# A tenth ring slot for the weights of experts, in space from a smaller DMA scratch and from the tile of router weights; weights in whole tiles

## The chip, the core and the metric

The kernel runs on one core of a Trainium2 chip. The metric is the device time of one execution in microseconds (us). Before the change three runs took 2025.5, 2029.56 and 2029.66 us, median 2029.56. Times inside an execution come from a profiled execution that took 2025.04 us.

## The reference

Two blocks on 512 tokens of width 1024, all in float32. The first mixes a chunked state-space layer and windowed attention, then adds a mixture of 64 experts; the second mixes neighbourhood attention and gated linear attention, then adds a squared-ReLU layer. The part that matters is the experts:

```python
group_logits = t @ w_router_group            # 8 groups
exp_logits = t @ w_router_expert             # 8 experts in each
g_sel = argmax(group_logits)
top_logit, top_local = top_k(exp_logits[g_sel], 2)
gate = softmax(top_logit) * softmax(group_logits)[g_sel]
def expert_block(xb, e):
    hid = silu(xb @ w_gate[e]) * (xb @ w_up[e])     # 1024 -> 512
    return hid @ w_down[e]                          # 512 -> 1024
y = sum over the two chosen experts of gate * expert_block(t, e)
```

Each token goes to two experts of one group. The weights of all 64 experts, 3 matrices of 2 MiB each, are read once: 403 MB of the 494 MB that the execution moves.

## The kernel before

Work in the first block ends with the product with `w_out` (`wout_tail`, L379), tile of 128 tokens by tile; behind each tile comes its share of the routing (`route_tile`, L786, with the router's weights `wr`, and `choose`, L854). Then `experts` (L963) goes over 32 pairs of experts. For a pair, with up to 64 tokens for each expert, PE multiplies with the two gate matrices (L986, two halves of PE's columns side by side), with the two up matrices, turns the result, and multiplies with the two down matrices; between up and down it adds earlier results back to their tokens (`combine`, L1181). The rows of tokens are fetched by GpSimd with an indirect transfer (`fetch`, L841) one or two pairs ahead.

Weights come through a ring. `ring` (L113) takes the next slot and issues loads on SP's queue (`load`, L140: `parts` pieces of equal size, all 128 partitions each; L149). A slot holds one matrix, 16 KiB in each partition. There are nine slots during the experts: three of `ringp` (numbers 0, 1, 6), two of `ring2` (2, 3), two in `A1` and `A2`, which held the first block's normed input (4, 5, named `w16x`), and two of `ring3` (7, 8). Tile k goes to slot k mod 9. `ring3` is opened in `moe` (L729) on the space of the closed pools of the first block (`small1`, `wsp1`, `mix1`), so its first loads wait for the last readers and writers there. Six tiles serve a pair, in the order gate, gate, up, up, down, down; tile numbers in this text count them from 0 to 191. SP's instructions run in order, so a load that waits holds all later ones back. The number of pieces `n` is 4 for experts 0 to 11 (tiles 0 to 35) and 2 after (tiles 36 to 183); expert 2's and 3's gate tiles (6 and 7) take 8; the last four gate and up tiles and the last two down tiles (184 to 187, 190, 191) go through `pair` (L131), which mixes the pieces of two tiles.

A tile program orders the instructions of each engine from their dependencies; a load into a slot waits for the readers of the slot's last content, and for an earlier transfer whose completion semaphore it takes over. Eight such semaphores, DMAHW0 to DMAHW7, serve the transfers of SP and ScalarE in turn.

At the end `Begin` (L1756) starts the second block inside the last pair: it loads `wv` into slot 6 (L1793), and `wsplit` (L152) casts it on ScalarE.

Of the kernel before, what the change touches and what calls it, by code (L numbers as in the profile page):

```python
# [6 lines left out]
FT = mybir.dt.float32  # L7
# [21 lines left out]
class Net:  # L29
# [6 lines left out]
    def setup(self, ctx):  # L36
        tc, nc = self.tc, self.nc
        self.per = ctx.enter_context(tc.tile_pool(name="per", bufs=1))
        self.ringp = ctx.enter_context(tc.tile_pool(name="ring", bufs=3))
        self.dram = ctx.enter_context(tc.tile_pool(name="dram", bufs=1, space=bass.MemoryType.DRAM))  # L40
        self.ps = ctx.enter_context(tc.tile_pool(name="ps", bufs=1, space=PSUM))
        self.rings = [self.ringp]

        per = self.per
        self.H = per.tile([P, NT, D], FT, name="H")
        ones = self.ones = per.tile([P, P], FT, name="ones")
        nc.gpsimd.memset(ones, 1.0)
        self.warm(AF.Sqrt)

        def tri(name, pattern, cmp, base=0, cm=0, fill=0.0, src=None, n=P):  # L50
            t = per.tile([P, n], FT, name=name)
            nc.gpsimd.affine_select(t, ones[:, :n] if src is None else src, pattern=pattern, compare_op=cmp,
                                    fill=fill, base=base, channel_multiplier=cm)
            return t
        self.ident = tri("ident", [[1, P]], OP.is_equal, 0, -1)
        self.upto = tri("upto", [[1, P]], OP.is_ge, 0, -1)
        self.after = tri("after", [[-1, P]], OP.is_gt, 0, 1)
        self.before = tri("before", [[1, P]], OP.is_gt, 0, -1)


        i = self.ins
        self.col = {}

        def columns(name, queue, names):
            rows = per.tile([P, P], FT, name="rows")
            nc.gpsimd.memset(rows, 0.0)
            r = 0
            for n, k in names:
                queue.dma_start(rows[r:r + k, :], dap(i[n], 0, [[P, k], [1, P]]))
                r += k  # L70
            p = self.psum()
            self.pin(nc.tensor.transpose(p[:, :P], rows, self.ident))
            cols = per.tile([P, r], FT, name="c" + name)
            nc.vector.tensor_copy(cols, p[:, :r])
            r = 0
            for n, k in names:
                self.col[n] = cols[:, r:r + k]
                r += k
        self.columns = columns
        columns("a", nc.scalar, (("norm_mix", 8),))  # L80
# [32 lines left out]
    def ring(self, shape, dma, parts=1):  # L113

        self.nring = getattr(self, "nring", -1) + 1
        n = [p.bufs for p in self.rings]
        m = self.nslots = sum(n) + (0 if self.held is None else 2)
        k = self.nring % m
        t = (self.held or {}).get(k)
        if t is None:  # L120

            p = self.rings[0 if self.held is None else (0, 0, 1, 1, 0, 0, 0, 2, 2)[k]]
            if self.held is not None and k in (4, 5):
                t = self.per.tile([P, 4096], FT, name="w16x", tag=("A1", "A2")[k - 4])
            else:
                t = p.tile([P, 4096], FT, name="w16", tag="w16")
            if self.held is not None:
                self.held[k] = t
        return self.load(t, shape, dma, parts)
# [300 lines left out]
    def attention1(self, small, pool, kp, wp, w_in, A, mixes, rsa, kv):  # L430
# [22 lines left out]
        for j in range(8):  # L453
# [31 lines left out]
            if j == 0:  # L485
                p = self.proj(kv[1], A)
                vT = kp.tile([P, T], FT, name="vT", tag="dT", bufs=1)
                self.copy(vT, p)
                p = self.psum()
                for c in range(NT):  # L490
                    nc.tensor.transpose(p[:, c * P:(c + 1) * P], vT[:, c * P:(c + 1) * P], self.ident)
                v = pool.tile([P, NT, P], FT, name="v", bufs=1)
                self.copy(v.rearrange("p c d -> p (c d)"), p)
                self.setup_rest()
                self.router_weights()
            nm = small.tile([P, 2, NT], FT, name="nm", bufs=2)
            nc.vector.tensor_scalar(nm, mx, -1.0, None, op0=OP.mult)
            for hh in range(2):
# [230 lines left out]
    def moe(self, keep, then=None):  # L729

        tc = self.tc
        with ExitStack() as ctx:

            self.nring, self.held = -1, {}
            self.rings = [self.ringp, self.ring2, ctx.enter_context(tc.tile_pool(name="ring3", bufs=2, reuse_waits="tile"))]
            with tc.tile_pool(name="experts", bufs=2, reuse_waits="tile") as pool:
                with ExitStack() as inner:
                    front = inner.enter_context(tc.tile_pool(name="front", bufs=2, reuse_waits="tile"))
                    self.experts(keep, pool, front, inner, then and (lambda: then(inner)))
            self.rings, self.held = [self.ringp], None  # L740
        self.show("h1m", self.H)

    def router_weights(self):
        nc, i, per = self.nc, self.ins, self.per
        g8 = self.g8 = per.tile([P, KT], FT, name="g8")
        nc.gpsimd.dma_start(g8, i["norm_ffn"][0].rearrange("(p j) -> p j", j=KT))
        wr = self.wr = per.tile([P, KT, 72], FT, name="wr")
        nc.gpsimd.dma_start(wr[:, :, :8], i["w_router_group"][0].rearrange("(j p) n -> p j n", p=P))
        nc.gpsimd.dma_start(wr[:, :, 8:], i["w_router_expert"][0].rearrange("(j p) n -> p j n", p=P))
        nc.gpsimd.tensor_tensor(wr, wr, self.col["norm_ffn"].unsqueeze(2).to_broadcast([P, KT, 72]), OP.mult)  # L750

    def route_start(self, keep, pool):
# [13 lines left out]
        self.ones16 = pool.tile([P, P], BF, name="ones16", bufs=1)  # L766
        nc.gpsimd.tensor_copy(self.ones16, self.ones)
        self.before16 = pool.tile([P, P], BF, name="before16", bufs=1)
        nc.gpsimd.tensor_copy(self.before16, self.before)
        self.lg = pool.tile([P, NT, 72], FT, name="lg", bufs=1)  # L770
        self.M = None
        self.ex = keep.tile([P, NT, 8], FT, name="ex")
# [190 lines left out]
    def experts(self, keep, pool, front, inner, then):  # L963
# [5 lines left out]
        wd = i["w_down"][0].rearrange("e (p j) n -> e p j n", j=4)  # L969

        def weights(e0):
            n = 4 if e0 < 12 else 2
            one = lambda shape, w, e: [self.ring(shape, w[e + s], 8 if e == 2 and w is wg else n) for s in range(2)]
            up, dn = [P, KT, 512], [P, 4, D]
            if e0 == 60:

                late.extend((lambda: one(dn, wd, 60), lambda: self.pair(dn, (wd[62], wd[63]))))
                return [(one(up, wg, 60), one(up, wu, 60), None),
                        (self.pair(up, (wg[62], wg[63])), self.pair(up, (wu[62], wu[63])), None)]
            return [(one(up, wg, e0), one(up, wu, e0), one(dn, wd, e0))]  # L980
# [7 lines left out]
        def chosen(q):  # L988

            us = slice(256 * (q % 2), 256 * (q % 2) + 256)  # L990
            km = front.tile([P, 2, NT], FT, name="km", bufs=1)
            V.tensor_scalar(km, self.keys, -4096.0 * (q // 2), None, op0=OP.add)
            for c in range(NT):
                eq = front.tile([P, 256], FT, name="eq", bufs=1)
                V.tensor_scalar(eq, it[:, us], km[:, 0, c:c + 1], None, op0=OP.is_equal)
                V.scalar_tensor_tensor(self.S0[:, c, :], it[:, us], km[:, 1, c:c + 1], eq, op0=OP.is_equal, op1=OP.add)

        def values(q):

# [519 lines left out]
    def gla_gates(self, pool, zT):  # L1519
# [8 lines left out]
        def block(name, src, scale):  # L1528
# [2 lines left out]
            nc.gpsimd.memset(t[0:64, 64:], 0.0)  # L1531
            nc.gpsimd.memset(t[64:, 0:64], 0.0)
            return t
        frm = tmp("frm")[:, :P]
        nc.gpsimd.affine_select(frm, self.ones, pattern=[[-1, P]], compare_op=OP.is_ge, fill=0.0, base=0, channel_multiplier=1)
        s = 1.0 / 16
        cum = (block("upto2", self.upto, s), block("from2", frm, s))
        rest = (block("after2", self.after, s), block("before2", self.before, s))
        mask = (block("mf", self.upto, 1.0), block("mb", self.after, 1.0))

        la = [one(f"la{d}", [P, NT, 256]) for d in range(2)]
# [214 lines left out]
class Begin:  # L1756
# [27 lines left out]
    def norms(self):  # L1784
# [11 lines left out]
        for c in range(NT):  # L1796
            for n in range(2):
                if n:
                    (nc.gpsimd if c == 1 else V).tensor_tensor(h[:, c, :], h[:, c, :], self.gf, OP.mult)
                x = self.pool.tile([P, D], BF, name="x2")  # L1800
                if n and c == 3:
                    V.tensor_tensor_reduce(x, h[:, c, :], h[:, c, :], 1.0, 0.0, OP.mult, OP.add, s[:, 1, c:c + 1])
                else:
                    net.behind.append(nc.scalar.activation(x, h[:, c, :], AF.Square, accum_out=s[:, n, c:c + 1]))

        V.tensor_scalar(s, s, 1.0 / D, None, op0=OP.mult)
# [6 lines left out]
def body(tc, ins, out, dbg=None, stage="all"):  # L1813
    with ExitStack() as ctx:
# [10 lines left out]
        if stage == "moe":  # L1825
            with ExitStack() as ctx2:
                keep = net.moe_pools(ctx2)
                with tc.tile_pool(name="route", bufs=2, side="right", reuse_waits="tile") as pool:
                    net.router_weights()
                    net.route_start(keep, pool)  # L1830
                    net.route(keep, lambda each: [each(c) for c in range(NT)])
                net.moe(keep)
# [35 lines left out]
```

## Time and profile before

| | |
|---|---|
| profiled execution | 2025.04 us |
| its span, first to last instruction | 2023.3 us |
| PE busy | 1928.0 us (95%) |
| VectorE (DVE) busy | 946.3 us (47%) |
| ScalarE (ACT) busy | 534.7 us (26%) |
| GpSimd (POOL) busy | 191.2 us (9%) |
| DMA moved | 494.24 MB, 244 GB/s over the span |
| SP's queue (q1) | 483.63 MB, 60.0% of 16 engines' span |
| GpSimd's transfers (q0) | 6.96 MB, 1.5% |
| mean granted PE clock | 0.989 |

A row of the timeline gives start, duration, engine (SPq is SP's DMA queue), the kernel's line, the operation, what it writes `<-` reads, the number of merged instructions, and in brackets how long the engine had been idle and what ended that. A row of waits gives total us, number of times, longest. A row of a DMA queue gives packets, MB and the share of the 16 DMA engines' time in the stretch. A row of a line gives the number of instructions, shortest/median/longest duration in ns, and the first and last start. Matmul ends are modelled, so a busy PE is not a PE at its peak.

### The profile page before, as it was taken

The numbers are of one execution on the slowest core, as the hardware profiler recorded it, in microseconds if no ns is written. First come the engines' busy times: TensorE is split into PE (matmuls) and PEld (weight loads), VectorE is DVE, ScalarE is ACT, GpSimd is POOL, SyncE is SP. The second block draws the span as 40 slices with busy tenths as digits, with TensorE's granted clock in tenths as the row PEclk, the third lists the DMA queues.
The fourth block names the chain that finished last, engine by engine and source line by source line (L and its number), as shares of the span: only waits on it lengthen the run. The fifth ranks groups of instructions, "written<-read, shape, count | busy, mean of one in ns | idle before, by whom it ended". The sixth has DMA issues, their size and how long they took to land. (4 is left out here: it accounts for less than half of the span.)

```text
span 2023.3 us, 24002 instructions
## 1 busy us (share of the span) xinstructions
PE 1928.0 (95%) x9535; PEld 1209.0 (60%) x9535; DVE 946.3 (47%) x1891; ACT 534.7 (26%) x900; POOL 191.2 (9%) x245
## 2 busy tenths in 40 slices
PE   7999999999999999999999899999999999999998
PEld 5788777734444344343343344348767788888886
DVE  6764667733543243253243243235656654444355
ACT  5773445311010000000000000024443343223232
POOL 5211333110000000000000000002201010000000
PEclk9999999999999999999999999999999999999999
DMA  7312022799999999999999999984212112313211
GB/s 204 115 43 83 32 81 97 268 343 415 415 425 425 424 424 424 424 424 425 424 423 423 421 424 422 422 335 87 92 42 84 43 52 84 125 48 119 103 64 42
DMA packets 114777, 494.24 MB, mean 244 GB/s; under 512 B 16492, under 2 KB 23091, under 8 KB 74984
## 3 DMA queue, kind: packets, MB, share of 16 engines
q1 hardware_dynamic: 107720, 483.63, 60.0%
q0 software_dynamic: 6352, 6.96, 1.5%
q10 hardware_dynamic: 592, 2.10, 0.3%
q8 instruction: 76, 1.25, 0.3%
q14 instruction: 37, 0.30, 0.0%
HBM read 500.68 MB, written 6.15 MB: 250 GB/s over the span
## 5 line engine op out<-in xcount | busy, mean ns | idle before, releaser
L986 PE MATMUL pj<-w,xg 128*64 128x512 f32 x1696 | 467.8, 603 | 47.1 <-DMA w<-in_w_up 45.8
L986 PEld LDWEIGHTS pj<-w,xg 128*64 128x64 f32 x1696 | 152.5, 139 | 334.0 <-issue 257.5
L159 DVE TENSOR_TENSOR wL<-w,wH 128x1024 fp32r<-128x1024 f32 x135 | 167.4, 1241 | 201.1 <-ACT wH L158 198.4
L158 ACT CAST wH<-w 128x1024 fp32r<-128x1024 f32 x136 | 142.3, 1048 | 336.3 <-PE pj L179 163.9
L1091 DVE SCALAR_TENSOR_TENSOR hid<-pj,slots,hid 128x512 f32<-128x512 f32 x30 | 22.5, 751 | 426.8 <-PE pj L986 412.4
L1190 DVE TENSOR_TENSOR H<-sc,H 128x512 f32<-128x512 f32 x248 | 156.5, 683 | 6.2 <-PE sc L1187 3.5
L986 PE MATMUL pj<-w16x,xg 128*64 128x512 f32 x352 | 153.7, 619 | 0.9 <-DMA w16x<-in_w_gate 0.9
L1187 PE MATMUL sc<-yH,ST 128*128 128x512 f32 x256 | 112.7, 440 | 0.6 <-DVE H L1190 0.6
L843 POOL DMA_INDIRECT rows<-hd,tok x31 | 31.7, 1022 | 817.1 <-DVE gates L837 574.3
L1100 ACT COPY hT<-tp 128x512 f32<-128x512 f32 x32 | 18.8, 587 | 339.9 <-PE tp L1098 339.9
L180 PE MATMUL pj<-n3H,wL 128*128 128x512 f32 (+1 forms) x272 | 103.6, 381 | 0.8 <-DVE wL L159 0.8
L178 PE MATMUL pj<-n3H,wH 128*128 128x512 f32 (+1 forms) x272 | 103.6, 381 | 0.0
L179 PE MATMUL pj<-n3L,wH 128*128 128x512 f32 (+1 forms) x272 | 103.5, 380 | 0.0
L178 PE MATMUL pj<-A,wH 128*128 128x512 f32 x240 | 97.3, 405 | 4.0 <-ACT wH L158 2.8
L1187 PE MATMUL sc<-yL,ST 128*128 128x512 f32 x252 | 99.9, 396 | 0.0
L178 PE MATMUL sc<-wH,mixH 128*128 128x512 f32 x252 | 98.5, 391 | 0.4 <-ACT wH L158 0.4
L179 PE MATMUL sc<-wL,mixH 128*128 128x512 f32 x252 | 98.4, 390 | 0.1
L180 PE MATMUL sc<-wH,mixL 128*128 128x512 f32 x252 | 98.2, 390 | 0.0
L179 PE MATMUL pj<-A,wH 128*128 128x512 f32 x240 | 96.8, 403 | 0.0
L180 PE MATMUL pj<-A,wL 128*128 128x512 f32 x240 | 96.2, 401 | 0.5 <-DVE wL L159 0.5
L986 PE MATMUL y<-w,hT 128*64 128x512 f32 x336 | 78.0, 599 | 0.7 <-DMA w<-in_w_down 0.7
L986 PE MATMUL tp<-w,hT 128*64 128x512 f32 x336 | 76.5, 592 | 0.0
(586 smaller groups left out, 3279.6 us busy)
## 6 DMA issues: line engine op xcount, KB each, us to landing
w<-in_w_up SPq DMA_DIRECT2D x88, 1024.0 KB, 20.8
w<-in_w_gate SPq DMA_DIRECT2D x84, 1024.0 KB, 19.6
w<-in_w_down SPq DMA_DIRECT2D x70, 1024.0 KB, 19.6
w16x<-in_w_down SPq DMA_DIRECT2D x32, 1024.0 KB, 20.2
w<-in_w_ff SPq DMA_DIRECT2D x16, 2048.0 KB, 7.8
w<-in_w_in SPq DMA_DIRECT2D x12, 2048.0 KB, 10.4
w<-in_w_up SPq DMA_DIRECT2D x40, 512.0 KB, 9.9
w16x<-in_w_gate SPq DMA_DIRECT2D x20, 1024.0 KB, 19.8
```

What stands on the lines that cost most here:

```text
L158: a = nc.scalar.copy(H, src)
L159: b = (engine or nc.vector).tensor_tensor(L, src, H.bitcast(FT), OP.subtract)
L178: m = mm(out, lH, rH, start=first, stop=False)
L179: mm(out, lH, rL, start=False, stop=False)
L180: mm(out, lL, rH, start=False, stop=last)
L843: self.nc.gpsimd.indirect_dma_start(out=rows, out_offset=None, in_=self.hd[:, :], in_offset=bass.IndirectOffsetOnAxis(ap=tok, axis=0), bou ...
L986: return self.pin(nc.tensor.matmul(*a, **k))
L1091: V.scalar_tensor_tensor(hid, pu, r, hid, op0=OP.mult, op1=OP.mult)
L1100: nc.scalar.copy(hT.rearrange("p j s -> p (j s)"), p)
L1187: m = nc.tensor.matmul(p, ST[:n, t * P:(t + 1) * P], y[:n], start=k == 0, stop=k == len(mms) - 1)
L1190: nc.vector.tensor_tensor(h[:, t, hs], p, h[:, t, hs], OP.add)
```

## The change

The ring gets a tenth slot: a third buffer of `ring3` (slot 9), so tile k goes to slot k mod 10. Its 16 KiB per partition come from a smaller scratch for GpSimd's transfers (4096 bytes of each partition; the default is 16384), from `wr`, which moves from the lasting pool into `small1`, and from smaller tiles: the triangle `before` is made where it is used, `eq` in `chosen` is written into `S0` itself, and the scratch output `x2` of the second block's norms has one buffer, not two (its last use writes `gf`). Loads come in 2 pieces for experts 0 to 7 (tiles 0 to 23) and in one piece for the others; `pair` and the 8 pieces of tiles 6 and 7 stay.

```diff
-            p = self.rings[0 if self.held is None else (0, 0, 1, 1, 0, 0, 0, 2, 2)[k]]
+            p = self.rings[0 if self.held is None else (0, 0, 1, 1, 0, 0, 0, 2, 2, 2)[k]]
...
-            self.rings = [self.ringp, self.ring2, ctx.enter_context(tc.tile_pool(name="ring3", bufs=2, reuse_waits="tile"))]
+            self.rings = [self.ringp, self.ring2, ctx.enter_context(tc.tile_pool(name="ring3", bufs=3, reuse_waits="tile"))]
...
-        wr = self.wr = per.tile([P, KT, 72], FT, name="wr")
+        wr = self.wr = pool.tile([P, KT, 72], FT, name="wr", bufs=1)
...
-        nc.gpsimd.tensor_copy(self.before16, self.before)
+        before = pool.tile([P, P], FT, name="before", bufs=1)
+        nc.gpsimd.affine_select(before, self.ones, pattern=[[1, P]], compare_op=OP.is_gt, fill=0.0, base=0, channel_multiplier=-1)
+        nc.gpsimd.tensor_copy(self.before16, before)
...
-            n = 4 if e0 < 12 else 2
+            n = 2 if e0 < 8 else 1
...
-                eq = front.tile([P, 256], FT, name="eq", bufs=1)
-                V.tensor_scalar(eq, it[:, us], km[:, 0, c:c + 1], None, op0=OP.is_equal)
-                V.scalar_tensor_tensor(self.S0[:, c, :], it[:, us], km[:, 1, c:c + 1], eq, op0=OP.is_equal, op1=OP.add)
+                S = self.S0[:, c, :]
+                V.tensor_scalar(S, it[:, us], km[:, 0, c:c + 1], None, op0=OP.is_equal)
+                V.scalar_tensor_tensor(S, it[:, us], km[:, 1, c:c + 1], S.bitcast(FT), op0=OP.is_equal, op1=OP.add)
...
-                x = self.pool.tile([P, D], BF, name="x2")
                 if n and c == 3:
-                    V.tensor_tensor_reduce(x, h[:, c, :], h[:, c, :], 1.0, 0.0, OP.mult, OP.add, s[:, 1, c:c + 1])
+                    V.tensor_tensor_reduce(self.gf, h[:, c, :], h[:, c, :], 1.0, 0.0, OP.mult, OP.add, s[:, 1, c:c + 1])
                 else:
+                    x = self.pool.tile([P, D], BF, name="x2", bufs=1)
...
-    nc = bacc.Bacc("TRN2", target_bir_lowering=False, num_devices=1)
+    nc = bacc.Bacc("TRN2", target_bir_lowering=False, num_devices=1, dynamic_dma_scratch_size=4096)
```

In `gla_gates` of the second block the triangle is made on GpSimd in the same way, one more select there and one fewer in the setup.

SP's queue where the ring is full for the first time. Before (`w_3921` is slot 7, `w_3930` slot 8, `w_3736` and `w_3741` slots 0 and 1; rows of 512 elements are 2 KiB in each partition, of 1024 4 KiB, and so on; in brackets what the load waits for):

```order
L149 DMA w_3921<-in_w_gate 128x512 [waits DMASW1_49,DMASW5_49,DMASW0_49,DMAHW4_49,DVE_49,Activation_49]
...
L149 DMA w_3930<-in_w_up 128x1024 [waits DMAHW5_49]
L149 DMA w_3930<-in_w_up 128x1024 [waits DMAHW6_49]
L149 DMA w_3930<-in_w_up 128x1024 [waits DMAHW7_49]
L149 DMA w_3930<-in_w_up 128x1024 [waits DMAHW0_49]
L149 DMA w_3736<-in_w_up 128x1024 [waits DMAHW1_49,PE_49]
L149 DMA w_3741<-in_w_down 128x1024 [waits DMAHW2_49,PE_49]
```

Now (`w_3905` is slot 7, `w_3914` slot 8, `w_3917` the new slot 9, `w_3736` slot 0):

```order
L148 DMA w_3905<-in_w_gate 128x512 [waits DMASW3_49,DMASW1_49,DMASW4_49,DMASW0_49,DMASW5_49,DVE_49,DMAHW1_49,PE_49,Activation_49]
...
L148 DMA w_3914<-in_w_up 128x2048 [waits DMAHW1_49]
L148 DMA w_3914<-in_w_up 128x2048 [waits DMAHW2_49]
L148 DMA w_3917<-in_w_up 128x2048 [waits DMAHW3_49]
L148 DMA w_3917<-in_w_up 128x2048 [waits DMAHW4_49]
L148 DMA w_3736<-in_w_down 128x2048 [waits DMAHW5_49,PE_49]
L148 DMA w_3736<-in_w_down 128x2048 [waits DMAHW6_49,PE_49]
```

Tile 9, the second `w_up` of pair 1, went to slot 0 and waited for PE; it now goes to slot 9 and waits for none of the engines, and tile 10 is the first that waits for PE. Slot 7's first load waits for PE too, as it did not.

SP's queue in the middle of the stage, before, two rows for each tile:

```order
L149 DMA w_3912<-in_w_up 128x2048 [waits DMAHW3_49,PE_49]
L149 DMA w_3912<-in_w_up 128x2048 [waits DMAHW4_49,PE_49]
L149 DMA w_3921<-in_w_down 128x2048 [waits DMAHW5_49]
L149 DMA w_3921<-in_w_down 128x2048 [waits DMAHW6_49,PE_49]
L149 DMA w_3930<-in_w_down 128x2048 [waits DMAHW7_49,PE_49]
L149 DMA w_3930<-in_w_down 128x2048 [waits DMAHW0_49,PE_49]
```

Now one row for each tile:

```order
L148 DMA w_3914<-in_w_up 128x4096 [waits DMAHW5_49,PE_49]
L148 DMA w_3917<-in_w_up 128x4096 [waits DMAHW6_49,PE_49]
L148 DMA w_3736<-in_w_down 128x4096 [waits DMAHW7_49,PE_49]
L148 DMA w_3739<-in_w_down 128x4096 [waits DMAHW0_49,PE_49]
L148 DMA w_3742<-in_w_gate 128x4096 [waits DMAHW1_49,PE_49]
```

Eight semaphores covered four tiles, and now cover eight.

ScalarE at the end of the last pair, before (`yH` is the last down product's first part, `n2H` the second block's input, `w_3912` holds `wv`):

```order
L171 ACTIVATE yH<-tp,mine 128x512
L171 ACTIVATE yH<-pj,mine 128x512 x2
L158 CAST wH<-w_3912 128x1024
L171 ACTIVATE n2H<-sc,both 128x512 x3
L171 ACTIVATE n2H<-y,both 128x512
```

Now, with `wv` in `w_3896`:

```order
L170 ACTIVATE yH<-tp,mine 128x512
L157 CAST wH<-w_3896 128x1024 x2
L170 ACTIVATE yH<-pj,mine 128x512 x2
L170 ACTIVATE n2H<-sc,both 128x512 x3
L170 ACTIVATE n2H<-y,both 128x512
```

The first two casts of `wv` stand ahead of the last two `yH`.

More of the change, by code (lines that the diff above doesn't have):

```diff
@@ L57, in setup @@
         self.after = tri("after", [[-1, P]], OP.is_gt, 0, 1)
-        self.before = tri("before", [[1, P]], OP.is_gt, 0, -1)
         i = self.ins
@@ L494, in attention1 @@
                 self.setup_rest()
-                self.router_weights()
+                self.router_weights(small)
             nm = small.tile([P, 2, NT], FT, name="nm", bufs=2)
@@ L741, in moe, with router_weights @@
         self.show("h1m", self.H)
-    def router_weights(self):
+    def router_weights(self, pool):
         nc, i, per = self.nc, self.ins, self.per
@@ L1533, in block @@
             return t
-        frm = tmp("frm")[:, :P]
+        frm, before = [tmp(n)[:, :P] for n in ("frm", "before")]
         nc.gpsimd.affine_select(frm, self.ones, pattern=[[-1, P]], compare_op=OP.is_ge, fill=0.0, base=0, channel_multiplier=1)
+        nc.gpsimd.affine_select(before, self.ones, pattern=[[1, P]], compare_op=OP.is_gt, fill=0.0, base=0, channel_multiplier=-1)
         s = 1.0 / 16
         cum = (block("upto2", self.upto, s), block("from2", frm, s))
-        rest = (block("after2", self.after, s), block("before2", self.before, s))
+        rest = (block("after2", self.after, s), block("before2", before, s))
         mask = (block("mf", self.upto, 1.0), block("mb", self.after, 1.0))
@@ L1828, in body @@
                 with tc.tile_pool(name="route", bufs=2, side="right", reuse_waits="tile") as pool:
-                    net.router_weights()
+                    net.router_weights(net.per)
                     net.route_start(keep, pool)
```

## The prediction

> **What bounds the kernel now.** I read the page first: the engines' shares, then the slices of the span.
>
> ```profile
> PE 1928.0 (95%) x9535; PEld 1209.0 (60%) x9535; DVE 946.3 (47%) x1891; ACT 534.7 (26%) x900; POOL 191.2 (9%) x245
> DMA  7312022799999999999999999984212112313211
> GB/s 204 115 43 83 32 81 97 268 343 415 415 425 425 424 424 424 424 424 425 424 423 423 421 424 422 422 335 87 92 42 84 43 52 84 125 48 119 103 64 42
> ...
> q0 software_dynamic: 6352, 6.96, 1.5%
> ```
>
> A slice is 50.6 us. PE looks full, but from slice 9 to slice 26 the DMA engines are full too, at a flat 415 to 425 GB/s: 192 tiles of 2 MiB (64 experts, three matrices of one tile each) pass there. Which of the two waits tells the bound; so next the waits of PE and of SP's queue over the whole span.
>
> ```profile
> PE pj L986 <- DMA w<-in_w_up: 45.8, 22, 3.4
> SPq L149 <- DMA w<-in_w_up: 200.0, 109, 3.7
> SPq L149 <- PE pj L986: 29.5, 25, 10.4
> ```
>
> PE waits for weights 22 times, about once per pair of experts, and always at `w_up`. SP hardly waits for PE to free a tile; it waits for an earlier DMA to land (200.0 us on `w_up` alone), since eight completion semaphores (DMAHW0 to 7 in the order above) let eight DMAs be out at once. The pace of PE shows in ScalarE's timeline, by the Silu that follows each gate product:
>
> ```profile
> 423.19 0.69 ACT L1088 ACTIVATE hid<-pj,slots 128x512 f32<-128x512 f32 x1 [6.78 <-DVE slots L831]
> 582.76 0.69 ACT L1088 ACTIVATE hid<-pj,slots 128x512 f32<-128x512 f32 x1 [6.18 <-PE pj L986]
> ...
> 637.65 0.69 ACT L1088 ACTIVATE hid<-pj,slots 128x512 f32<-128x512 f32 x1 [6.60 <-PE pj L986]
> 1305.19 0.69 ACT L1088 ACTIVATE hid<-pj,mine 128x512 f32<-128x512 f32 x1 [6.35 <-PE pj L986]
> ```
>
> The first two are six pairs apart: 159.57 / 6 = 26.6 us a pair, while PE lives on the tiles loaded ahead. The last two are 22 pairs apart: 667.54 / 22 = 30.3 us. So PE could do a pair in 26.6 us and gets its 12.58 MB only every 30.3. From about 600 us the weight stream is the bound, and what ends the stage is when that stream began, where it paused, and how long a tile takes.
>
> **The tile's time, by the size of its pieces.** Before, tiles 0 to 35 come in 4 pieces (rows of 4 KiB), tiles 36 to 183 in 2 (8 KiB). The queue's bytes in the stretches 460 to 555 us (4 pieces) and 570 to 1290 us (2 pieces):
>
> ```profile
> q1 hardware_dynamic: 10658, 38.80, 100.8%
> ```
>
> ```profile
> q1 hardware_dynamic: 41410, 301.57, 99.8%
> ```
>
> 38.80 MB / 95 us = 408 GB/s, 5.135 us a tile; 301.57 / 720 = 419 GB/s, 5.007 us a tile. Both are saturated (the last column), so the difference, 0.128 us, is the price of the smaller pieces. SP's issue times say the same in another way:
>
> ```profile
> 461.38 0.33 SPq L149 DMA_DIRECT2D w<-in_w_gate  x1
> 555.39 0.33 SPq L149 DMA_DIRECT2D w<-in_w_gate  x1
> 566.03 0.33 SPq L149 DMA_DIRECT2D w16x<-in_w_down  x1
> 1293.10 0.33 SPq L137 DMA_DIRECT2D w16x<-in_w_gate  x1
> ```
>
> The first two are tiles 18 and 36: 94.01 / 18 = 5.223 us. The last two are tiles 40 and 184: 727.07 / 144 = 5.049 us. Difference 0.174. I take the mean of the two readings, 0.151 us a tile from 4 pieces to 2. No trace shows a row of 16 KiB or a DMA of 2 MiB in this stream. If the price is one per piece or per row (each engine's part then costs a fixed bit more), it halves whenever the pieces double: from 2 pieces to 1 it is 0.075 us a tile (0.064 to 0.087). That is my value; the lower bound is zero, and below zero I see no row that speaks for it, since the one step that is measured went the other way.
>
> **The change, part by part.**
>
> Tiles 10 to 23 go from 4 pieces to 2: 14 x 0.151 = 2.1 us. Tiles 24 to 35 from 4 to 1: 12 x (0.151 + 0.075) = 2.7 us. Tiles 36 to 183 from 2 to 1: 148 x 0.075 = 11.1 us. All three lie on the path, because the queue never rests there. Tiles 184 to 187, 190 and 191 keep their pieces.
>
> [...]
>
> The tenth tile. Before, the stream's head looks so (columns: busy of PE, PEld, DVE, ACT, POOL, then PE clock, DMA share, GB/s), with the two waits of SP in it and PE's rows that end them:
>
> ```profile
> 396.00:400.00 4.00, 4.00 (x22) 2.99 (x21) 3.58 (x16) 0.81 (x2) 0.00 (x0) 1.00 0.09 35
> 408.00:412.00 4.00, 3.12 (x6) 1.07 (x4) 2.83 (x14) 0.42 (x2) 0.00 (x0) 0.63 0.99 375
> 412.00:416.00 4.00, 2.92 (x15) 1.44 (x16) 1.94 (x8) 3.28 (x5) 0.00 (x0) 0.94 0.31 126
> 416.00:420.00 4.00, 4.00 (x20) 1.29 (x18) 0.14 (x1) 0.40 (x2) 1.84 (x4) 1.00 0.55 140
> 440.00:444.00 4.00, 4.00 (x28) 2.48 (x26) 2.27 (x5) 0.69 (x1) 0.00 (x0) 1.00 0.98 352
> ```
>
> ```profile
> SPq L149 <- DVE H L399: 7.1, 1, 7.1
> SPq L149 <- PE pj L986: 11.2, 2, 10.4
> ```
>
> ```profile
> 398.62 0.74 DVE L399 SCALAR_TENSOR_TENSOR H<-tp,rs,H 128x512 f32<-128x512 f32 x1
> 401.82 1.01 PE L800 MATMUL y<-wr,xT 128*128 128x72 f32 x8
> 414.81 7.09 PE L986 MATMUL pj<-w,xg 128*64 128x512 f32 x32 [0.35 <-DVE xg L1015]
> 417.19 0.38 SPq L149 DMA_DIRECT2D w<-in_w_down  x1
> ```
>
> Against 375 GB/s, 396 to 400 us lost 3.6 us of DMA time and 412 to 420 lost 5.2 us: the first because slot 7 lies on memory of the mixer's pools, which DVE's last L399 frees at 399.4, the second because nine tiles were full and tile 9 had to wait for PE's first gate product (10.4 us of waiting). With a tenth slot, tile 9 need not wait. But the change also puts `wr` into `small1`, on which slot 7 now lies, and the new order lists a wait for PE there: L800 reads `wr` until 402.8, so slot 7 starts 3.4 us later and the first gap grows to 7.0. After it come three tiles, 15.5 us, to 418.5; tile 10's first half is free after half of the product, 414.81 + 3.55 = 418.4, and arrives perhaps a microsecond later. So 8.8 us idle becomes about 8: the tenth tile's own gain here is 0.8 us, not the 5.0 us of a tile. After it, 440 to 448 us ran at some 350 instead of 408 GB/s while SP waited for PE, worth 1.2 us; ten slots should spare that. Together 2.0 us (0 to 5.0).
>
> The end. Whole tiles make PE wait for a whole pair where it began with three quarters:
>
> ```profile
> 1307.97 7.08 PE L986 MATMUL pj<-w,xg 128*64 128x512 f32 x30 [2.17 <-DMA w<-in_w_up]
> 1337.47 1.94 PE L986 MATMUL y<-w,hT 128*64 128x512 f32 x8 [0.17 <-DMA w<-in_w_down]
> 1339.90 1.50 PE L986 MATMUL y<-w,hT 128*64 128x512 f32 x5 [0.49 <-DMA w<-in_w_down]
> 1349.50 7.09 PE L986 MATMUL pj<-w,hT 128*64 128x512 f32 x32
> ```
>
> The down product of pair 30 catches the last half of tile 189 (`w_down` of expert 61) at 1339.9; by then 8 of its 32 matmuls, and a few before the first wait, are done, a quarter to a third of the 7.1 us that such a product takes. With tile 189 in one piece none of them can be: 1.8 to 2.4 us come to lie behind the landing, and I take 2.4, about half a tile's time. Earlier waits of this kind cost nothing: PE has 30.3 - 26.6 = 3.7 us to spare in each pair.
>
> The rest is hidden. POOL's new `before` is one more 128x128 select: the old like one, L1535, took 0.29 us at 1463.7, and PE reads `before2` first at 1536.8. The comparison that wrote `eq` writes the same 256 columns into `S0`, on an engine that is busy 47%.
>
> ```profile
> L1535 POOL TENSOR_SCALAR_AFFINE_SELECT frm<-ones x1: 293/293/293, 1463.7 to 1463.7; 128x128 f32<-128x128 f32 x1
> L1612 PE MATMUL sc<-la,before x16: 275/275/275, 1536.9 to 1566.6; 128*128 128x128 f32 x16
> 1340.22 6.25 SPq L1793 DMA_DIRECT2D w<-in_w_in  x1
> w<-in_w_in SPq DMA_DIRECT2D x1, 512.0 KB, 12.7
> ```
>
> Two casts of `wv` move ahead of ScalarE's last `yH` (third order above). `yH` would wait behind them if `wv` came late; the second piece was issued at 1340.2 and landed 12.7 us on, at 1352.9, and `yH` is due only when the product of 1349.50 has ended, so there are 3 us of cover, and if they fail, ScalarE's lateness delays PE's next products one for one. The smaller scratch could make GpSimd wait for room for its transfers; they are 1.5% of the DMA's time, and nothing on the path waits for them long. I put zero on both, with 0 to 2 us for the range.
>
> The sum: 2.1 + 2.7 + 11.1 + 2.0 - 2.4 = 15.5 us. The profiled execution took 2025.04 us (span 2023.3), the three runs 2025.5, 2029.56 and 2029.66: two near 2025.3, two near 2029.6, of which the trace is one of the lower. The sum holds against either; from their middle, 2027.3, it gives 2011.8, and I say 2012. From the profiled execution alone it would be 2009.5, from the median 2014.1. A measurement of this kernel can tell some 0.2%, 4 us, from no change.
>
> **The rivals.**
>
> First, whole tiles move no faster than halves. For it: nothing in the trace has rows above 8 KiB, and 424 GB/s is flat over 700 us. Against it: the step from 4 to 8 KiB. The third term goes and the second shrinks to 12 x 0.151 = 1.8: 2.1 + 1.8 + 2.0 - 2.4 = 3.5 us, so 2021.5 from the profiled execution, 2023.8 from the middle. Chance 0.17. [...]
>
> Second, and slower: the ring runs dry. A whole tile's slot is handed back only when PE is through with all of it, so the next DMA into it goes out later. The down pair is held longest: it lands while PE is still in the up product, and is done 7.1 + 5.3 + 7.1 = 19.5 us after that product began (5.3 us is what three products of 7.1 leave of a pair's 26.6). If that left no tile in flight once per pair of experts, the queue would rest from issue to first data, about 1.4 us (SP issued again at 417.2, and 140 GB/s from 416 to 420 is 375 from 418.5 on): 148 / 6 x 1.4 = 35 us, less the gain of 15.5, so 2027.3 + 19 = 2046. Against it: in 19.5 us four tiles land, so of ten, four hold data and six, 30 us of transfer, are still on their way. It decides only if PE falls behind by six tiles. Chance 0.06.
>
> Third, PE takes part of it back. After a wait PE starts slowly:
>
> ```profile
> 914.67 1.12 PE L986 MATMUL pj<-w,xg 128*64 128x512 f32 x1 [3.43 <-DMA w<-in_w_up]
> 917.90 0.59 PE L986 MATMUL pj<-w,xg 128*64 128x512 f32 x1
> ```
>
> Three steps took 3.2 us where three take 1.3, some 1.9 us lost after 3.43 us of waiting. With whole tiles the gate and the down product may come to wait like this too: 26.6 + 3 x 1.9 = 32.3 us a pair, more than the 29.9 that the stream would give. But a PE that is late finds its tiles there and doesn't wait, so this cannot last; I allow half of the third term: 2012 + 5.5 = 2017. Chance 0.07.
>
> **How the numbers follow.** The forecast has 0.70, the rivals 0.17, 0.06 and 0.07. For the range: the upper readings throughout (0.174 and 0.087 a tile, 5.0 us at the head, nothing at the end) give 2.4 + 3.1 + 12.9 + 5.0 = 23.4, so 2025.04 - 23.4 = 2001.6; the first rival with the upper pair of runs gives 2029.6 - 3.5 = 2026. Range 2001 to 2025, which leaves out the dry ring and the outer edges. Faster by over 0.2%: all of the forecast, 0.06 of the first rival (its 3.5 us lie just under the bound) and 0.05 of the third: 0.81. Within: 0.10 + 0.02 = 0.12. Slower: the second and a trace of the first, 0.07.
>
> **What the profile after would show.** The queue's rate in the middle of the stage at 424 to 427 GB/s of its own, 429 to 431 in all, and the gate's Silus 29.9 us apart instead of 30.3. Slot 7 issued after 402.8, no wait of 10 us for PE behind it, and no gap at 412 to 420. At the end a wait of PE for `w_down` of 1 to 3 us. The forecast is wrong if the rate stays at 424 (first rival), if SP waits for PE once per pair (second), or if PE's waits for DMA all but vanish while the period stays near 30 (third).

## The result and the profile after

Five runs of the changed kernel took 2011.66 to 2018.33 us, median 2013.55; five of the kernel before, beside them, 2025.5 to 2031.96, median 2029.56. The ratio is 0.9929, with a 95% interval of 0.9917 to 0.9942: 14.4 us faster (11.8 to 16.8, each end by 2029.56). The profiled execution took 2011.66 us, its span 2010.0.

The page of the kernel after, engines first, then GB/s in 40 slices of 50.3 us:

```profile
PE 1924.2 (96%) x9535; PEld 1209.5 (60%) x9535; DVE 942.0 (47%) x1891; ACT 535.8 (27%) x900; POOL 193.7 (10%) x246
...
GB/s 208 113 43 84 16 80 116 251 376 426 430 429 429 428 428 430 429 428 430 428 430 428 429 429 429 417 298 69 92 43 84 43 53 84 126 57 111 109 60 42
```

The plateau rose from 424 to 429. PE's busy time hardly moved (1928.0 before), so what went is waiting. SP's queue in the same two stretches as before, 460 to 555 us (halves for the first third of the bytes, then whole tiles) and 570 to 1290 us (whole tiles), with one row of its issues:

```profile
q1 hardware_dynamic: 3726, 40.16, 99.5%
```

```profile
q1 hardware_dynamic: 21121, 305.24, 99.3%
...
w<-in_w_gate SPq DMA_DIRECT2D x36, 2048.0 KB, 38.9
...
rows<-hd,tok POOLq DMA_INDIRECT x24, 12.8
```

The packets (first number) fell from 41410 to half, for more bytes. 305.24 MB in 720 us is 424 GB/s of the queue's own, 4.947 us a tile of 2.097 MB instead of 5.007. A gate tile lands 38.9 us after its issue (median), which is 7.9 tiles' time: the queue holds some eight tiles at once.

The waits over the whole span, PE's for weights and then SP's:

```profile
PE pj L988 <- DMA w<-in_w_up: 29.8, 17, 2.5
PE pj L988 <- DMA w16x<-in_w_up: 8.3, 4, 3.6
```

```profile
SPq L148 <- PE tp L988: 204.3, 30, 12.5
SPq L148 <- PE pj L988: 200.6, 63, 8.3
...
SPq L148 <- DMA w<-in_w_up: 88.2, 33, 4.0
```

PE still waits at `w_up` once in most pairs, 38.1 us in all instead of 45.8. SP has changed its reason: before, it waited for earlier DMAs to land, now it waits 405 us for PE to hand back slots, though the queue stays full. ScalarE's Silus after the gate products give the pace:

```profile
423.42 0.69 ACT L1090 ACTIVATE hid<-pj,slots 128x512 f32<-128x512 f32 x1 [6.72 <-DVE slots L833]
...
583.05 0.69 ACT L1090 ACTIVATE hid<-pj,slots 128x512 f32<-128x512 f32 x1 [6.18 <-PE pj L988]
...
1294.20 0.69 ACT L1090 ACTIVATE hid<-pj,mine 128x512 f32<-128x512 f32 x1 [6.18 <-PE pj L988]
...
1314.81 0.69 ACT L1090 ACTIVATE hid<-pj,mine 128x512 f32<-128x512 f32 x1 [9.75 <-PE pj L988]
```

The first (pair 0) and the second (pair 6) stand where they stood, within 0.3 us; that of pair 30 comes 11.0 us earlier and the last, of pair 31, 12.7 us (1327.54 before). Nearly all the gain is made between 583 and 1315 us, where the stream is the bound. From the first Silu to the last is 891.4 us, 904.4 before; the experiments below use this distance, since their first Silus lie up to 6 us apart (422.93 to 428.92), from work ahead of the experts.

The head, in slices of 4 us with the columns as before, then SP's waits there (330 to 460 us), and PE's last reading of `wr`:

```profile
396.00:400.00 4.00, 4.00 (x21) 3.04 (x21) 3.21 (x16) 0.59 (x1) 0.00 (x0) 1.00 0.04 17
408.00:412.00 4.00, 2.88 (x6) 1.07 (x5) 2.74 (x16) 0.42 (x2) 0.00 (x0) 0.70 1.01 341
412.00:416.00 4.00, 2.92 (x14) 1.30 (x14) 1.80 (x6) 2.99 (x5) 0.00 (x0) 0.87 1.01 424
416.00:420.00 4.00, 4.00 (x22) 1.42 (x20) 0.36 (x3) 0.69 (x2) 1.84 (x4) 1.00 1.01 426
440.00:444.00 4.00, 4.00 (x28) 2.37 (x26) 1.98 (x5) 0.69 (x1) 0.00 (x0) 1.00 0.95 371
```

```profile
SPq L148 <- PE pj L988: 29.1, 8, 8.3
...
SPq L148 <- DVE H L398: 7.6, 1, 7.6
...
SPq L148 <- PE y L802: 3.5, 1, 3.5
```

```profile
402.24 1.01 PE L802 MATMUL y<-wr,xT 128*128 128x72 f32 x8
```

Slot 7 waits for DVE, as before, and then 3.5 us more for PE's product with `wr`; the gap at 412 to 420 is gone (424 and 426 instead of 126 and 140). At the end of the stage PE's matmuls show no wait for `w_down`, but its weight loads (PEld) do:

```profile
1295.24 7.08 PE L988 MATMUL pj<-w,xg 128*64 128x512 f32 x30 [0.26 <-DMA w<-in_w_up]
...
1307.67 7.09 PE L988 MATMUL pj<-w16x,xg 128*64 128x512 f32 x32
1314.59 7.04 PE L988 MATMUL pj<-w,xg 128*64 128x512 f32 x32
...
1323.50 4.31 PE L988 MATMUL y<-w,hT 128*64 128x512 f32 x15
...
1331.60 0.50 PE L988 MATMUL sc<-ST,yH 128*128 128x512 f32 x1
```

```profile
1323.49 0.19 PEld L988 LDWEIGHTS y<-w,hT 128*64 128x64 f32 x2
1324.59 0.20 PEld L988 LDWEIGHTS y<-w,hT 128*64 128x64 f32 x4 [0.90 <-DMA w<-in_w_down]
```

The same two places before:

```profile
1339.89 0.20 PEld L986 LDWEIGHTS y<-w,hT 128*64 128x64 f32 x4 [1.37 <-DMA w<-in_w_down]
```

```profile
1345.19 0.50 PE L986 MATMUL sc<-ST,yH 128*128 128x512 f32 x1
```

The product that begins at 1323.50 is the down product of pair 30, which waited twice for tile 189 before. Now two of its 32 matmuls are done when the first load that needs tile 189 waits 0.90 us for it, until 1324.59. PE's matmul rows show no gap there, since the ends of matmuls are modelled. From the last landing to the row behind the product (`sc`) it is 7.0 us (1324.59 to 1331.60), and it was 5.3 before (1339.89 to 1345.19).

### The profile page after: what moved, and what is told of

Read it like the earlier page. It is cut to its first block, busy times and chain, and to the rows that moved or that the text cites. A ratio compares the mean times of both kernels' runs of the same rounds, so it can differ in the third digit from the quotient of the medians.

```text
span 2010.0 us, 23650 instructions
## 1 busy us (share of the span) xinstructions
PE 1924.2 (96%) x9535; PEld 1209.5 (60%) x9535; DVE 942.0 (47%) x1891; ACT 535.8 (27%) x900; POOL 193.7 (10%) x246
## 5 line engine op out<-in xcount | busy, mean ns | idle before, releaser
L988 PE MATMUL pj<-w,xg 128*64 128x512 f32 x1632 | 385.3, 607 | 30.5 <-DMA w<-in_w_up 29.8
L988 PEld LDWEIGHTS pj<-w,xg 128*64 128x64 f32 x1632 | 128.9, 140 | 278.9 <-issue 229.3
L988 PE MATMUL pj<-w16x,xg 128*64 128x512 f32 x416 | 96.1, 593 | 8.3 <-DMA w16x<-in_w_up 8.3
L988 PE MATMUL y<-w,hT 128*64 128x512 f32 x400 | 92.4, 599 | 0.0
L988 PE MATMUL tp<-w,hT 128*64 128x512 f32 x400 | 90.9, 592 | 0.0
## 6 DMA issues: line engine op xcount, KB each, us to landing
w16x<-in_w_down SPq DMA_DIRECT2D x10, 2048.0 KB, 38.9
```

The costliest lines, as they stand in the source:

```text
L988: return self.pin(nc.tensor.matmul(*a, **k))
```

## The experiments

The theory at this point: the gain is 2 us from the slot and the rest from longer rows. Rivals: the slot kept the queue full, so the slot is the gain; the size of the DMA counts and not that of the row; PE's own pace limits what is left.

**The slot alone, the pieces alone.** The first kernel keeps the slot and goes back to the old pieces; the second has nine slots and the old tiles and scratch, with the new pieces; the third has ten slots and two pieces for every tile.

```diff
-            n = 2 if e0 < 8 else 1
+            n = 4 if e0 < 12 else 2
```

> The change with its ten slots, but with the pieces as before (4 for tiles 0 to 35, 2 after). My theory gives the tenth slot 2.0 us by itself (0 to 5), and the end no loss: about 2 us under the kernel before, 14 us over the changed kernel, and the queue at 419 GB/s between 570 and 1290 us. The rival that the slot carries the gain (more room to load ahead all the way) would put it within 4 us of the changed kernel.

```profile
q1 hardware_dynamic: 41424, 301.68, 99.8%
```

Ratio to the kernel before 0.999 (0.9979 to 1.0), first to last Silu 901.3 us. Two us by the timing (0 to 4.3), 3.0 by the trace; in the middle the stream moves what it moved before.

```diff
-            n = 4 if e0 < 12 else 2
+            n = 2 if e0 < 8 else 1
```

> The kernel before with its nine slots, and only the pieces as in the change (2 for tiles 0 to 23, 1 after). If the size of the pieces carries the gain and nine slots are enough to keep the queue full, 13 to 14 us under the kernel before (2.1 + 2.7 + 11.1 - 2.4), the queue at 424 GB/s between 570 and 1290 us. The rival that whole tiles need the tenth slot (the ring of nine runs dry, since a slot comes back only when PE has read all of it) gives a queue under 419 GB/s or a DMA share under 1.00 there, and a time no better than before.

```profile
q1 hardware_dynamic: 21010, 305.19, 99.3%
...
w<-in_w_gate SPq DMA_DIRECT2D x39, 2048.0 KB, 28.7
```

```profile
SPq L149 <- PE pj L986: 391.6, 86, 13.5
SPq L149 <- PE tp L986: 301.8, 30, 12.5
```

Ratio 0.9946 (0.9934 to 0.9959), 894.8 us between the Silus: 11 us under the kernel before, where 13 to 14 were expected, and 3.4 us behind the change, by the timing and by the Silus. With nine slots SP waits still longer for PE, 693 us, and fewer tiles are out (28.7 us from issue to landing for gate tiles, 33 for down tiles), yet the queue moves the same 305 MB. So neither the tenth slot nor anything else is needed to keep whole tiles flowing: the ring that runs dry does not exist here, not even with one slot less.

```diff
-            n = 2 if e0 < 8 else 1
+            n = 2
```

> The change, but with 2 pieces for every tile instead of 1 from tile 24 on. My theory: it loses the step from 2 to 1 on 160 tiles, 160 x 0.075 = 12.0 us, and gets back the 2.4 us of the end: 9.6 us slower than the changed kernel (6 to 13), 6 us faster than before. If whole tiles gave nothing, no slower than the changed kernel.

```profile
q1 hardware_dynamic: 41403, 301.48, 99.8%
```

Ratio 0.9965 (0.9952 to 0.9978), 900.4 us. From here to the change, 160 tiles (24 to 183) go from two pieces to one: 0.0036 of 2029.56 is 7.3 us by the timing (about 3.7 either way, from the two intervals), 9.0 us between the Silus, and 160 x 0.060 = 9.6 us by the queue's bytes.

**The end.** The change, with halves for all six tiles of experts 60 and 61: gate and up (180 to 183), and the down tiles 188 and 189, for which the forecast charged 2.4 us.

```diff
-            n = 2 if e0 < 8 else 1
+            n = 2 if e0 < 8 or e0 == 60 else 1
```

> The change, but with 2 pieces for the tiles of experts 60 and 61 (180 to 183, 188, 189), the last whole tiles. My theory: the down product of pair 30 starts with the first half again, 1.8 to 2.4 us earlier, so 2 us under the changed kernel, against 0.4 us for six tiles in smaller pieces. The rival that PE's own chain, not the last landing, sets the end gives no difference.

```profile
1329.94 0.20 PEld L988 LDWEIGHTS y<-w,hT 128*64 128x64 f32 x4 [0.75 <-DMA w<-in_w_down]
```

```profile
1335.24 0.50 PE L988 MATMUL sc<-ST,yH 128*128 128x512 f32 x1
```

Ratio 0.9929 (0.9914 to 0.9943), the change's own; the difference of two such ratios is known to some 4 us, so the timing cannot decide on 2. The trace shows what the theory said. Counted from the first Silu of each kernel (428.92 and 423.42), the last half of tile 189 lands where the whole tile landed (901.0 and 901.2 us), but the row behind the product begins at 906.3 instead of 908.2: 1.9 us earlier. The Silus, 889.7 us from first to last, 1.7 less than the change, tell of another part of the edit: with halves in tiles 180 to 183 the wait at `w_up` of pair 30 (0.26 us in the change) is gone, and the last two Silus stand 19.3 us apart instead of 20.6. Each number comes from one execution. So whole tiles at the end cost about 1.9 us in the trace, which the timing can neither confirm nor exclude.

**Quarters.** Ten slots and four pieces in the middle of the stage, to see the third point of the line in one and the same place of the program.

```diff
-            n = 2 if e0 < 8 else 1
+            n = 4
```

> Ten slots, four pieces (rows of 4 KiB) for every tile up to 183. Theory A, a fixed price per row, 0.062 us a piece: 0.128 us more than halves for each of 148 tiles, 19 us, less 2 for the slot, so 17 us slower than before, ratio 1.008, and 294 MB (408 GB/s) in the stretch 570 to 1290 us. Theory B, the 408 GB/s of quarters in the early stretch came from its place in the program and not from the rows: 301.6 MB and a ratio of 0.999, as the slot alone. Theory C, four pieces with eight semaphores leave only two tiles in flight and the queue runs dry now and then: clearly under 294 MB and slower than 1.01.

```profile
q1 hardware_dynamic: 80539, 293.27, 101.0%
```

Ratio 1.0076 (1.0063 to 1.0089), 916.3 us. 5.149 us a tile; with 5.008 (halves, ten slots) and 4.947 (whole) the steps are 0.140 for two pieces fewer and 0.062 for one: a fixed price for each piece, 0.07 and 0.06 us, and not the stretch of the program. Theory A. A little of the 0.140 may be short pauses, as in Theory C: the slices of this kernel's page stand at 411 to 416 GB/s in the stretch, with two at 406 and 400.

**Row or DMA?** Halving the number of pieces doubles both the row and the DMA. Two kernels keep one and change the other. The first brings a tile in one DMA with two rows of 8 KiB for each partition; the matrix' rows then stand in another order, so the products are of other numbers.

```diff
+                raw = self.ins["w_gate" if w is wg else "w_up" if w is wu else "w_down"][0]
+                return [self.ring(shape, raw[e + s].rearrange("(h p j) n -> p h j n", h=2, p=P), -2) for s in range(2)]
```

> The change, but a tile of experts 8 to 59 comes as one DMA of 2 MiB in 256 rows of 8 KiB (two per partition, from the two halves of the matrix in memory) instead of 128 rows of 16 KiB; the rows of the matrix then stand in another order, so the products are other numbers of the same shape and time. Theory A, the price is one per row: as halves, 301.6 MB in the stretch 570 to 1290 us, ratio to the kernel before 0.9965. Theory B, the price is one per DMA: as the change, 305.2 MB, ratio 0.993.

```profile
q1 hardware_dynamic: 38819, 302.47, 99.8%
...
w<-in_w_down SPq DMA_DIRECT2D x38, 2048.0 KB, 36.5
```

The DMAs have their 2048 KB, the packets are nearly as many as with halves (38819 to 41403; most of the difference is packets under 512 B, of which the stretch has 5056 and 7347 in all queues, since there are half as many DMAs). Ratio 0.9976 (0.9965 to 0.9987), 900.6 us: as halves, not as the change. The other way round, rows of 16 KiB in two DMAs, was first tried by lower and upper 64 partitions.

```diff
-            n = 2 if e0 < 8 else 1
+            n = 2 if e0 < 8 else -2
...
+            m = P // -parts
+            for k in range(-parts):
+                self.nc.sync.dma_start(v[k * m:(k + 1) * m], dma[k * m:(k + 1) * m])
```

> The change, but from tile 24 on a tile comes in two DMAs split by partition (64 partitions each) instead of one: rows stay 16 KiB, two DMAs a tile. Theory A, the price is one per row of a partition (the stretch 570 to 1290 us moved 301.6 MB in rows of 8 KiB and 305.2 MB in rows of 16 KiB): as the change, 305 MB there, ratio to the kernel before 0.993. Theory B, the price is one per DMA: as halves, 301.6 MB there, ratio 0.9965.

```profile
GB/s 218 42 68 34 102 130 316 416 219 224 225 220 220 222 224 227 238 277 260 304 326 350 375 349 314 340 339 306 186 145 81 35 68 69 77 102 102 68 102 34
```

```profile
q1 hardware_dynamic: 13373, 175.27, 99.7%
```

Neither theory: ratio 1.2128 (1.2101 to 1.2156), with runs from 2454 to 2772 us. From the slice in which the split begins the stream falls from 416 to some 220 GB/s, half of the 429 of the change, while the DMA engines are 99.7% busy: a packet takes 16 x 720 x 0.997 / 13373 = 0.86 us there on average, and 0.54 in the change by the same division. Each DMA writes only 64 partitions there, and they are neighbours; which of the two costs the rate, this run doesn't tell. The next kernel therefore keeps 64 partitions in each DMA and splits by even and odd ones.

```diff
-                self.nc.sync.dma_start(v[k * m:(k + 1) * m], dma[k * m:(k + 1) * m])
+                self.nc.sync.dma_start(v[k::-parts], dma[k::-parts])
```

> The change, but from tile 24 on a tile comes in two DMAs, the even partitions and the odd partitions (64 rows of 16 KiB each), where the earlier experiment gave one DMA the lower and one the upper 64 partitions and fell to 220 GB/s. Theory A, what hurt there was that a DMA wrote only one half of the partitions, neighbours of each other: here every DMA covers the whole range, and the queue is back at 424 GB/s, 305 MB in the stretch, ratio 0.993. Theory B, a DMA over 64 partitions is slow whichever they are: about 220 to 300 GB/s and a ratio of 1.2.

```profile
q1 hardware_dynamic: 23281, 304.56, 99.3%
```

Ratio 0.9946 (0.9927 to 0.9966), 891.2 us. Theory A: a DMA over 64 partitions is not slow by itself. The four together (MB that the queue moved from 570 to 1290 us, us between the Silus):

```
                 one DMA a tile      two DMAs a tile
rows of 16 KiB   305.24   891.4      304.56   891.2   (odd and even)
rows of  8 KiB   302.47   900.6      301.48   900.4
```

The row's length makes 2.8 to 3.1 MB and 9 us, the number of DMAs 0.7 to 1.0 MB and nothing that the Silus show (the order in which memory is read differs within each line of the table too, and was not tried by itself). Most of the price hangs on the row.

The packets' own durations in the traces (medians, 570 to 1290 us) show where it lies: 159 ns for 4 KiB (quarters), 309 for 8 KiB (halves, and the same with two rows in one DMA), 611 for 16 KiB (the change, and the same with odd and even partitions). Two packets of 8 KiB take 7 ns longer than one of 16 KiB, two of 4 KiB 9 ns longer than one of 8. A tile has 128 rows of 16 KiB, on average eight for each of the 16 DMA engines: 8 x 7 = 56 ns a tile from halves to whole tiles and 16 x 9 = 144 ns from quarters to halves, against the 62 and 140 of the bytes.

**Slot 7's new wait.** The router's weights moved to the upper end of `mix1`, where no slot lies, so that slot 7 needs no reader of `wr`.

```diff
-                self.router_weights(small)
+                self.router_weights(self.mixp)
```

> The change, with the router's weights at the upper end of another pool of the first block, on which no slot of the ring lies. Slot 7 then waits for DVE's last addition only, as before the change, and is issued 3 to 3.5 us earlier than now. Theory A (the prediction's working): the three tiles behind it are through earlier, but tile 10 still waits for half of PE's first product, so the 3 us come back as a gap before tile 10: gain over the change 0 to 0.5 us, ratio to the kernel before 0.993. Rival: the whole stream starts 3 us earlier and everything ends 3 us earlier: ratio 0.9914.

Slices of this kernel, and its longest wait of SP at the head:

```profile
412.00:416.00 4.00, 2.47 (x6) 0.99 (x5) 3.08 (x18) 0.42 (x2) 0.19 (x1) 0.79 1.00 389
416.00:420.00 4.00, 3.27 (x12) 1.87 (x12) 1.31 (x5) 2.89 (x5) 0.00 (x0) 0.50 1.02 430
420.00:424.00 4.00, 4.00 (x18) 1.22 (x16) 1.01 (x5) 0.79 (x2) 1.84 (x4) 0.85 0.66 277
```

```profile
SPq L148 <- PE pj L988: 30.5, 7, 12.7
```

Ratio 0.9934 (0.9919 to 0.9949), 890.9 us. This execution has its first Silu at 428.69, 5.3 us later than the change's. Slot 7's wait for `wr` is gone, and in its place a gap opens at 420 to 424 and SP's longest wait for PE's product grows from 8.3 to 12.7 us: the 3.5 us are given back before tile 10, as the forecast's arithmetic had it. Tile 10 is issued 4.6 us ahead of the first Silu in both kernels (at 424.05 here, at 418.77 in the change).

**PE's own pace.** Only the first half of the down tiles of experts 12 to 59 is loaded; the products read what the slot held.

```diff
+        if parts < 0:
+            self.nc.sync.dma_start(v[:, :shape[1] // 2], dma[:, :shape[1] // 2])
+            return v
```

> The change, but of each down tile of experts 12 to 59 only the first half is loaded (the second half of the slot keeps what it held), so a pair costs 10.49 MB instead of 12.58: 24.7 us of stream at 424 GB/s. All matmuls stay. Theory A (the prediction's): PE needs 26.6 us a pair, so the gate's Silus come 26.6 us apart, PE's waits for weights go, and 24 pairs save 3.4 us each, some 80 us. Rival: PE's own pace in the middle of the stage is slower than in its first pairs (30.04 us less 1.8 us of waits is 28.2 us): Silus 28 us apart and some 45 us saved.

```profile
640.91 0.69 ACT L1093 ACTIVATE hid<-pj,slots 128x512 f32<-128x512 f32 x1 [6.15 <-PE pj L991]
...
1229.54 0.69 ACT L1093 ACTIVATE hid<-pj,mine 128x512 f32<-128x512 f32 x1 [6.18 <-PE pj L991]
```

Ratio 0.9595 (0.9581 to 0.9609), 68 us faster than the change, and PE waits for no weights in the stage. These Silus are 22 pairs apart: 26.76 us a pair, what PE did in its first pairs, and not 28; over the 22 pairs that are saved against 30.04 this makes 72 us. The 30.04 us a pair of the change ((1294.20 - 693.46) / 20, from pair 10 to pair 30) hold 1.8 us of waiting (35.4 us of PE's waits from 690 to 1290 us, in 20 pairs); the other 1.5 us go when the waits go, so they belong to them. PE could still give 3.3 us a pair.

**All of it.** The router's weights in `mix1`, halves for experts 60 and 61, whole tiles from tile 12 on.

```diff
-            n = 2 if e0 < 8 else 1
+            n = 2 if e0 < 4 or e0 == 60 else 1
```

> The change with the router's weights in the other pool, whole tiles from expert 4 on (tile 12) instead of 8 (tile 24), and halves for the down tiles of experts 60 and 61. By the price of a piece, 12 tiles less 0.06 us each, 0.7 us; the other two gave 0 in the timing and 0.5 and 1.7 us between the first and the last Silu in the trace. Together 0.7 to 2.9 us faster than the change, ratio to the kernel before 0.992; the rival is that nothing is left there, 0.993.

Ratio 0.993 (0.9913 to 0.9948), 889.8 us. No faster than the change by the timing; 1.6 us in the trace is what the halves at the end had shown alone, and the row behind the down product of pair 30 begins 906.4 us after the first Silu, as it did with those halves alone (906.3). No version was found that is measurably better.

## Why the prediction was right, and where it was not

**What bounds it.** Right. The gain lies where the stream is the bound, the first six pairs kept their time, and with a sixth of the bytes gone PE falls back to its 26.76 us a pair. From pair 8 to pair 30 the Silus are 29.9 us apart, as forecast (30.3 before).

**The step from two pieces to one** (0.075 us a tile, 11.1 us for tiles 36 to 183). The mechanism held, a fixed price for each row; the size was the low reading of the two. The queue's bytes now give 0.060, so 8.9 us for those tiles. The forecast averaged that reading's 0.128 with SP's issue times, 0.174. Issue times of two tiles say when a slot came free and a semaphore was met, and both ends move with that; the bytes that a saturated queue moves in 720 us are the better measure, and alone would have given 0.064. The packets' durations give 0.056.

**The step from four pieces to two** (0.151). In one place of the program 0.140 by the bytes; (1.0076 - 0.9965) x 2029.56 / 174 tiles = 0.129 by the timing, 0.144 by the packets' durations. What it gave in tiles 10 to 35, where the change makes it, is less sure: the kernel with the slot alone and the one with halves differ there, by 5 us in the timing (3.4 either way) and by 1.0 between the Silus, against 26 x 0.151 = 3.9.

**The tenth slot** (2.0 us). Right within what can be told: 2.0 (0 to 4.3) by the timing of the slot alone, 3.4 beside nine slots with whole tiles, and each part of it was seen, the wait for `wr`, the closed gap, and that undoing the one brings back the other. SP's wait for PE is 3.5 us, 3.4 were worked out.

**The end** (-2.4 us). The mechanism held, and the size was 1.7. Tile 189 still lands inside the down product of pair 30, and behind its landing lie 7.0 us instead of 5.3, because only two matmuls can go ahead of it and not ten. The halves at the end put 5.3 us behind the landing again (1329.94 to 1335.24). The two waits of before were no chance of one execution: a weight load of that product waits for `w_down` with the slot and the old pieces (0.3 us), with halves everywhere (0.3), with nine slots and whole tiles (0.9) and with quarters (3.4) too. The sign that the forecast named, 1 to 3 us of waiting, came just under its range (0.90).

**The sum.** 2.1 + 2.7 + 11.1 + 2.0 - 2.4 = 15.5 against 14.4 (11.8 to 16.8) by the timing. In the two traces the last landing comes 15.3 us earlier (1339.89 to 1324.59), where the four gains make 17.9, and 1.7 us more lie behind it, where 2.4 were charged: 13.6 at the row behind the product (1345.19 to 1331.60). So the gains were put 2.6 us too high and the charge 0.7 too high, and the second takes back a part of the first. By the reading of the bytes alone the gains would have been 1.8 + 2.3 + 9.5 + 2.0 = 15.6. The 2012 also started from 2027.3, between the runs known then; from the median of 2029.56 the same sum gives 2014.1, 0.5 us from the measured one.

**The rivals.** Whole tiles that move no faster: fell, since the same stretch moves 305.24 MB instead of 301.57, 1.2% more. The queue moves 424 and all queues together 429 GB/s. The dry ring: fell, by the kernel with nine slots. But the sign that the forecast named for it, SP waiting for PE once a pair, did come, 93 waits and 405 us, and meant nothing: with 7.9 tiles out a wait of SP is covered by what is queued, and the sign should have been the queue's share. PE that takes it back: fell. 1.5 us a pair do go to slow starts after waits, but as much before (30.34 us a pair from pair 10 to pair 30, less 26.76 and 2.0 of waiting), so it is no share of the gain. In the forecast's two rows four steps lie between 914.67 and 917.90, not three, so the slow start there cost 3.2 - 4 x 0.43 = 1.5 us and not 1.9.

## What to carry to other kernels

Where a queue is saturated, count the rows of a partition: here each further row per partition cost about 0.06 us (1.2%) in a tile of 2 MiB, down to one row of 16 KiB, and splitting a transfer into pieces is worth that only where somebody uses the first piece before the last has landed, as the last down product does here (1.9 us in the trace). When a transfer must be split without shorter rows, split it into odd and even partitions and not into lower and upper halves: here the first moved 304.56 MB in 720 us and the second 175.27, against 305.24 unsplit. Price a step from bytes per time of a full queue, and ask of every gap that is closed which wait comes next, since 3.5 us at slot 7 were worth nothing behind the wait for PE at tile 10. And read the waits of the weight loads beside those of the matmuls: here the last wait for weights shows in them alone.

## What the runs showed of the hardware

Two DMAs over 64 neighbouring partitions each, issued one behind the other on one queue, took it from 429 to 220 GB/s at first and to some 300 to 375 later in the same run; why neighbours cost that much and why it recovers, no run shows. Odd and even partitions lose nothing but 0.2% of the queue's bytes (304.56 MB against 305.24).

GpSimd's gathers beside the stream get slower as its rows get longer: 7.1 us to landing (median of 24, from 570 to 1290 us) beside rows of 4 KiB, 9.1 to 9.8 beside 8 KiB, and 12.2 to 13.0 beside 16 KiB, with nine slots and the old scratch (12.9) as with ten and the new. It follows the row and not the DMA: 9.8 with one DMA in rows of 8 KiB, 12.2 with two in rows of 16. Beside the stream split into lower and upper halves, rows of 16 KiB too, it is 19.3 (median of 12). No wait for them shows in that stretch, so no run shows what their slowness costs where a wait for them is on the path.
